# Wider modulation products on VectorE, and a final norm worked by column groups, in a two-layer diffusion trunk

## The chip, the cores and the metric

The kernel runs on one core of one Trainium2 chip. The metric is the device time of one execution in microseconds (us). The time of the kernel before is 1545.48 us, the median of three runs.

## The reference, cut to what matters

Two groups of tokens, 128 context tokens (TP) and 256 latent tokens (TS), 384 columns in all (T), pass through two layers with the same weights. D is 1024, so a token's features lie in KD = 8 blocks of 128 partitions. Each layer is

```
m  = modulation(c, w_ada[l], b_ada[l])                  # 9 vectors of 1024 for each of the two groups
x += 0.5 * m[2] * swiglu(norm(x) * (1 + m[1]) + m[0])   # FFN, d_ff 2816
x += m[5] * (mixers(norm(x) * (1 + m[4]) + m[3]) @ w_out)
x += 0.5 * m[8] * swiglu(norm(x) * (1 + m[7]) + m[6])   # FFN
modulation(c) = silu(c) @ w_ada + b_ada                 # c: (1024,) for each group
y = rms_norm(x, final_norm)                             # once, behind the second layer
```

## The kernel before, in words

Activations are held transposed: features on partitions, the 384 tokens as columns, the two groups as column ranges (`GROUPS`). Every large weight tile is loaded into one of five `raw` buffers by a DMA that SyncE's queue issues, split into a high part by ScalarE (L200) and a low part by VectorE (L201), and multiplied by TensorE in three passes (`mm3`, L210). A `raw` buffer is free again when its low part has been written.

An FFN (`ffn`) runs over 22 blocks of the hidden width in two halves of 11: gate and up products (`g`, `u`), an activation, then for each of the 8 output blocks `j` a down product `dn`, an add into `x` (`add_x`, L290), the scaled input of the next sublayer (`scaled`, L264 and L265) and the square for its norm (`Sumsq.add`, L237). A list `SIDE` says beside which of the 38 steps of an FFN the modulation vectors of later sublayers are worked out. One vector is done by TensorE (`ada_pe`), fifteen by VectorE (`ada_dve`): for each of 8 weight tiles `rawada` [128, 1024], loaded through the same five `raw` buffers, VectorE multiplies the tile by silu(c) of both groups, spread over all partitions, and sums along the columns. The products themselves are thrown away into a PSUM tile `junk`; the sums are kept. L174 does this in pieces of 512 columns, four for each tile. The spread silu(c), `requests`, is loaded anew for each of the four FFNs by `requests_of` (L162, activation at L163), into buffers of the group "S" (8 buffers of 512 columns), which the mixers use too.

The mixers of a layer hold their small weights in a buffer `lw` [128, 2048] of their own (L452), read by several streams of the mixers and, ahead of them, by `narrow` (L466), which makes `wkr`.

The order of the instructions on each engine is set when the program is built, by a scheduler that goes by priority (the order of the program text) and by its own model of when operands are ready. Buffers of one tag are handed out again when their last reader is done. The calls that select a ScalarE table by name (`log_exp`, `act_table`) are pinned in program order; where an activation needs another table than the one loaded, a table load is put ahead of it.

The end: `Sumsq.end` (L243) sums the squares over partitions with a product with ones (L245 for the sum of seven blocks, L247 for the last), `rstd_of` takes Ln and Exp (L221, L222) over all 384 columns, L1099 forms `y` for the 8 blocks, and L1101 stores two blocks at a time from SyncE's queue.

Of the kernel before, what the change touches and what calls it, by code (L numbers as in the profile page):

```python
# [15 lines left out]
P = 128  # L16
D = 1024
# [27 lines left out]
def trunk(ctx, tc, a):  # L45
# [108 lines left out]

    requests = {}

    def requests_of():

        for v in range(2):
            for z in range(2):  # L160
                t = slot("S", "req", (512,))
                nc.sync.dma_start(out=t, in_=a["c"][v:v + 1, z * 512:(z + 1) * 512].to_broadcast([P, 512]))  # L162
                S.activation(t, t, AF.Silu)  # L163
                requests[v, z] = t
        yield

    def ada_dve(l, n):

        sums = sb.tile([P, KD, 2, 2], F32, tag="adasum", name=nm("adasum"), bufs=2)
        for k in range(KD):  # L170
            t = load_w(a["w_adaT"][l, n, k], "ada")
            for v in range(2):
                for z in range(2):
                    V.scalar_tensor_tensor(xbank("junk")[:, 0, :], t[:, z * 512:(z + 1) * 512], 1.0, requests[v, z],  # L174
                                           op0=ALU.mult, op1=ALU.mult, accum_out=sums[:, k, v, z:z + 1])
            if k == KD - 1:
                m = mods[l][:, n * 8:(n + 1) * 8, :]
                V.tensor_tensor(m, sums[:, :, :, 0], sums[:, :, :, 1], op=ALU.add)
                V.tensor_tensor(m, m, bada[:, l, n * 8:(n + 1) * 8].unsqueeze(2).to_broadcast([P, KD, 2]), op=ALU.add)
# [39 lines left out]
    def rstd_of(dst, acc, n):  # L219

        S.activation(dst, acc, AF.Ln, bias=epsb, scale=1.0 / n)  # L221
        S.activation(dst, dst, AF.Exp, scale=-0.5)  # L222
        return dst

    class Sumsq:
# [5 lines left out]
        def add(self, k):  # L231
# [3 lines left out]
            else:  # L235
                sq = one("sq")
                S.activation(sq, x[k], AF.Square)  # L237
# [5 lines left out]
        def end(self):  # L243
            b = bank("ms")
            PE.matmul(b[:, :T], ones, self.acc, start=True, stop=not self.apart)  # L245
            if self.apart:
                PE.matmul(b[:, :T], ones, self.last, start=False, stop=True)  # L247
            return rstd_of(sb.tile([P, T], F32, tag="rstd", name=nm("rstd"), bufs=1), b[:, :T], D)
# [39 lines left out]
    def add_x(k, b, gt):  # L288
        for g, cs in GROUPS:
# [3 lines left out]
    def ffn(l, i, rstd, ab, nxt, side, hook=None, given=(), h=None):  # L293
# [7 lines left out]
        for half in range(2):  # L301
# [41 lines left out]
            for j in range(KD):  # L343
# [8 lines left out]
                add_x(j, b, gt)  # L352
# [76 lines left out]
    def mixers(l, rstd, gt, ab, nxt):  # L429
# [22 lines left out]
        lw = sb.tile([P, 2048], F32, tag="lw", name=nm("lw"), bufs=1)  # L452
# [630 lines left out]
    for l in range(NL):  # L1083
# [10 lines left out]
        ssq = ffn(l, 1, rstd, coefs_of(l, 2), before(l + 1, 0), lambda: side(SIDE[2 * l + 1]))  # L1094
# [156 lines left out]
```

## Time and profile before

| what | value |
|---|---|
| time, median of 3 runs | 1545.48 us (1545.38 to 1546.63) |
| profiled execution, its own time | 1547.53 us |
| its span, first to last instruction | 1545.1 us |
| TensorE busy | 1506.9 us, 98% of the span |
| VectorE busy | 1183.4 us, 77% |
| ScalarE busy | 752.6 us, 49% |
| moved by DMA | 257.33 MB, mean 167 GB/s |

All times are on the profile's clock, which starts at the first instruction. A busy share is that of the whole span; the kernel has an opening (0 to 53 us), four FFNs, two mixers and a tail behind the last down product, and each has limits of its own.

### The profile page before, as it was taken

To read this page: it belongs to the slowest core of one execution; us is meant where nothing else is said; L and a number is where in the kernel's file an instruction comes from. 1 tells how busy PE (TensorE), PEld (TensorE's weight loads), DVE (VectorE), ACT (ScalarE), POOL (GpSimd) and SP (SyncE) were. 2 spreads that over 40 slices of the span, in tenths; PEclk is the share of its full clock that TensorE was granted. 3 is DMA by queue.
4 is the path that set the end of the run, shared out by engine and by line. 5 is a ranking of instruction groups with operands and counts; after the bars stand their busy time and mean duration, and the time that the engine had idled before them with its cause. 6 is when DMAs were issued, how large, how long until landed. Compare 5 with 4: busy or idle time off the path is not lost.

```text
span 1545.1 us, 26749 instructions
## 1 busy us (share of the span) xinstructions
PE 1506.9 (98%) x10120; PEld 1423.9 (92%) x10120; DVE 1183.4 (77%) x2683; ACT 752.6 (49%) x1348; POOL 100.1 (6%) x122
## 2 busy tenths in 40 slices
PE   8999999999999999999999999999999999999997
PEld 5999999997778999999989999999877799999996
DVE  5879998969947988987987799785896599544433
ACT  5732333456788642333454323345677874323331
POOL 1000000100221000000100000001014010000001
PEclk9999999999999999999999999999999999999999
DMA  9877766641134465765645576555221255444331
GB/s 368 270 244 226 245 219 198 209 147 61 49 99 141 151 210 185 245 225 167 195 163 168 173 238 233 181 174 164 72 65 54 65 166 176 150 150 143 112 102 60
DMA packets 83025, 257.33 MB, mean 167 GB/s; under 512 B 9680, under 2 KB 11184, under 8 KB 82512
## 3 DMA queue, kind: packets, MB, share of 16 engines
q1 hardware_dynamic: 81744, 254.14, 50.5%
q8 instruction: 80, 1.31, 0.3%
q0 software_dynamic: 1152, 1.48, 0.3%
q14 instruction: 49, 0.40, 0.1%
HBM read 252.53 MB, written 2.26 MB: 165 GB/s over the span
## 4 chain that ended last, share of the span: by engine, by line
PE 83%; DVE 10%; DMA 3%; ACT 3%; issue 2%; SPq 0%; DVEq 0%; ACTq 0%
PE u L210 22%; PE g L210 22%; PE dn L210 19%; PE in L210 8%; PE out L210 3%; DVE junk L174 2%; PE po L424 1%; DMA rawada<-in_w_adaT 1%; PE sc L391 1%; DVE logu L201 1%; PE first L210 1%; DVE hl L265 1%; DVE loin L201 1%; DMA rawgu<-in_w_gu 1%; DVE x L290 1%
## 5 line engine op out<-in xcount | busy, mean ns | idle before, releaser
L174 DVE SCALAR_TENSOR_TENSOR junk<-rawada,req 128x512 f32<-128x512 f32 x480 | 339.3, 707 | 35.3 <-DMA rawada<-in_w_adaT 25.6
L200 ACT ACTIVATE higu<-rawgu 128x1024 fp32r<-128x1024 f32 (+1 forms) x178 | 186.5, 1050 | 289.9 <-PE u L210 92.8
L210 PE MATMUL g<-h,higu 128*128 128x384 f32 x1136 | 290.6, 335 | 2.0 <-ACT g L329 2.0
L210 PE MATMUL u<-h,higu 128*128 128x384 f32 x1136 | 288.7, 334 | 2.1 <-DVE x L290 1.4
L201 DVE TENSOR_TENSOR logu<-rawgu,higu 128x1024 fp32r<-128x1024 f32 (+1 forms) x178 | 215.2, 1211 | 36.3 <-PE g L210 18.6
L210 PE MATMUL dn<-ah,hidn 128*128 128x384 f32 x704 | 236.1, 335 | 0.2 <-ACT hh L264 0.2
L210 PE MATMUL dn<-al,hidn 128*128 128x384 f32 x704 | 235.9, 335 | 0.0
L210 PE MATMUL dn<-ah,lodn 128*128 128x384 f32 x704 | 235.9, 335 | 0.0
L200 ACT ACTIVATE hidn<-rawdn 128x768 fp32r<-128x768 f32 (+1 forms) x128 | 101.4, 792 | 250.9 <-PE dn L210 68.1
L210 PEld LDWEIGHTS g<-h,higu 128*128 128x128 f32 x1136 | 204.6, 188 | 6.0 <-ACT g L329 2.8
L210 PEld LDWEIGHTS u<-h,higu 128*128 128x128 f32 x1136 | 204.7, 188 | 3.4 <-issue 2.1
L210 PE MATMUL g<-h,logu 128*128 128x384 f32 x568 | 189.8, 334 | 0.0
L210 PE MATMUL u<-h,logu 128*128 128x384 f32 x568 | 189.8, 334 | 0.0
L201 DVE TENSOR_TENSOR lodn<-rawdn,hidn 128x768 fp32r<-128x768 f32 (+1 forms) x128 | 113.4, 886 | 30.5 <-issue 17.0
L210 PEld LDWEIGHTS dn<-ah,hidn 128*128 128x128 f32 x704 | 132.1, 188 | 0.5 <-ACT hh L264 0.5
L210 PEld LDWEIGHTS dn<-ah,lodn 128*128 128x128 f32 x704 | 132.1, 188 | 0.0
L210 PEld LDWEIGHTS dn<-al,hidn 128*128 128x128 f32 x704 | 132.1, 188 | 0.0
L239 POOL TENSOR_TENSOR ssq<-ssq,sq 128x384 f32<-128x384 f32 x42 | 46.5, 1106 | 1152.6 <-DVE hl L265 747.3
L210 PE MATMUL in<-hh,hiin 128*128 128x386 f32 x304 | 107.7, 354 | 0.0
L210 PEld LDWEIGHTS g<-h,logu 128*128 128x128 f32 x568 | 106.6, 188 | 0.0
L210 PEld LDWEIGHTS u<-h,logu 128*128 128x128 f32 x568 | 106.6, 188 | 0.0
L210 PE MATMUL in<-hl,hiin 128*128 128x386 f32 x304 | 106.3, 350 | 0.0
(312 smaller groups left out, 2433.7 us busy)
## 6 DMA issues: line engine op xcount, KB each, us to landing
rawgu<-in_w_gu SPq DMA_DIRECT2D x170, 512.0 KB, 4.3
rawada<-in_w_adaT SPq DMA_DIRECT2D x120, 512.0 KB, 3.8
rawdn<-in_w_dn SPq DMA_DIRECT2D x64, 384.0 KB, 3.6
rawdn<-in_w_dn SPq DMA_DIRECT2D x64, 320.0 KB, 3.0
rawin<-in_w_in SPq DMA_DIRECT2D x38, 512.0 KB, 3.7
rawout<-in_w_out SPq DMA_DIRECT2D x32, 256.0 KB, 2.7
ada<-in_w_ada SPq DMA_DIRECT2D x16, 384.0 KB, 7.3
rawada<-in_w_ada SPq DMA_DIRECT2D x8, 512.0 KB, 4.3
```

Source lines behind the costliest of these rows:

```text
L174: V.scalar_tensor_tensor(xbank("junk")[:, 0, :], t[:, z * 512:(z + 1) * 512], 1.0, requests[v, z], op0=ALU.mult, op1=ALU.mult, accum_out=s ...
L200: S.activation(hi, raw, AF.Copy)
L201: V.tensor_tensor(lo, raw, hi, op=ALU.subtract)
L210: i = PE.matmul(out, wt, xt, start=first and n == 0, stop=last and n == 2)
L239: (V if self.n == KD - 1 else G).tensor_tensor(self.acc, self.acc, sq, op=ALU.add)
L265: V.scalar_tensor_tensor(hl[:, k, cs], x[k][:, cs], at[:, k, g:g + 1], hh[:, k, cs], op0=ALU.mult, op1=ALU.subtract)
L290: V.scalar_tensor_tensor(x[k][:, cs], b[:, cs], gt[:, k, g:g + 1], x[k][:, cs], op0=ALU.mult, op1=ALU.add)
L391: PE.matmul(sc[:, u, :nk], q_of(u, blk), k_of(u, blk), start=True, stop=True)
L424: PE.matmul(bo[64 * u:64 * u + 64, :P], v_of(u, kt), pt[:, u, i * P:(i + 1) * P], start=(i == 0), stop=(i == len(kts) - 1))
```

## The change

`requests_of` loads the spread vectors for both groups into one tile of 2048 columns and applies Silu once. This tile has the tag "wide", with one buffer, and the mixers' `lw` takes its buffer from the same tag. L174 multiplies 1024 columns at once, so there are two products for each weight tile, their thrown-away result covers both banks of `junk`, and the addition of the two halves' sums falls away. In the last FFN, the last `add_x` takes the 256 latent columns first, the last square, the ones-products, Ln and Exp go by column group (latent first, Ln and Exp pinned in this order), the first pair of blocks of `y` goes by column group, `y` lies in buffers of the group "H", and the stores alternate between SyncE's and ScalarE's queue, the last pair as two single blocks.

```
+    def wide(s):
+        return sb.tile([P, 2048], F32, tag="wide", name=nm(s), bufs=1)
...
     def requests_of():
+        t = wide("req")
         for v in range(2):
-            for z in range(2):
-                t = slot("S", "req", (512,))
-                nc.sync.dma_start(out=t, in_=a["c"][v:v + 1, z * 512:(z + 1) * 512].to_broadcast([P, 512]))
-                S.activation(t, t, AF.Silu)
-                requests[v, z] = t
+            requests[v] = t[:, v * D:(v + 1) * D]
+            nc.sync.dma_start(out=requests[v], in_=a["c"][v:v + 1, :].to_broadcast([P, D]))
+        S.activation(t, t, AF.Silu)
...
     def ada_dve(l, n):
-        sums = sb.tile([P, KD, 2, 2], F32, tag="adasum", name=nm("adasum"), bufs=2)
+        sums = sb.tile([P, KD, 2], F32, tag="adasum", name=nm("adasum"), bufs=2)
...
             for v in range(2):
-                for z in range(2):
-                    V.scalar_tensor_tensor(xbank("junk")[:, 0, :], t[:, z * 512:(z + 1) * 512], 1.0, requests[v, z],
-                                           op0=ALU.mult, op1=ALU.mult, accum_out=sums[:, k, v, z:z + 1])
+                V.scalar_tensor_tensor(xbank("junk").rearrange("p a b -> p (a b)"), t, 1.0, requests[v],
+                                       op0=ALU.mult, op1=ALU.mult, accum_out=sums[:, k, v:v + 1])
...
-                V.tensor_tensor(m, sums[:, :, :, 0], sums[:, :, :, 1], op=ALU.add)
-                V.tensor_tensor(m, m, bada[:, l, n * 8:(n + 1) * 8].unsqueeze(2).to_broadcast([P, KD, 2]), op=ALU.add)
+                V.tensor_tensor(m, sums, bada[:, l, n * 8:(n + 1) * 8].unsqueeze(2).to_broadcast([P, KD, 2]), op=ALU.add)
...
-    def rstd_of(dst, acc, n):
-        S.activation(dst, acc, AF.Ln, bias=epsb, scale=1.0 / n)
-        S.activation(dst, dst, AF.Exp, scale=-0.5)
+    def rstd_of(dst, acc, n, pinned=False):
+        keep = tc.keep_in_program_order if pinned else lambda i: i
+        keep(S.activation(dst, acc, AF.Ln, bias=epsb, scale=1.0 / n))
+        keep(S.activation(dst, dst, AF.Exp, scale=-0.5))
...
         def add(self, k):
...
-                S.activation(sq, x[k], AF.Square)
+                for _, cs in reversed(GROUPS) if self.apart and self.n == KD - 1 else ((0, slice(0, T)),):
+                    S.activation(sq[:, cs], x[k][:, cs], AF.Square)
         def end(self):
...
+            groups = GROUPS[::-1] if self.apart else ((0, slice(0, T)),)
+            bs = [bank("ms") for _ in groups]
+            for b, (_, cs) in zip(bs, groups):
+                PE.matmul(b[:, cs], ones, self.acc[:, cs], start=True, stop=not self.apart)
+            for b, (_, cs) in zip(bs, groups):
+                if self.apart:
+                    PE.matmul(b[:, cs], ones, self.last[:, cs], start=False, stop=True)
+                rstd_of(rstd[:, cs], b[:, cs], D, self.apart)
...
     def ffn(l, i, rstd, ab, nxt, side, hook=None, given=(), h=None):
...
-                add_x(j, b, gt)
+                add_x(j, b, gt, GROUPS[::-1] if ssq.apart and half == 1 and j == KD - 1 else GROUPS)
...
     def mixers(l, rstd, gt, ab, nxt):
...
-        lw = sb.tile([P, 2048], F32, tag="lw", name=nm("lw"), bufs=1)
+        lw = wide("lw")
...
     rstd = ssq.end()
-    for k in range(KD):
-        if k % 2 == 0:
-            y = slot("M", "y", (2, T))
-        V.scalar_tensor_tensor(y[:, k % 2, :], x[k], fnorm[:, k:k + 1], rstd, op0=ALU.mult, op1=ALU.mult)
-        if k % 2 == 1:
-            nc.sync.dma_start(out=a["o_y"][:, k - 1:k + 1, :], in_=y)
+    y = [slot("H", "y", (2, T)) for _ in range(KD // 2)]
+    for n, cs in ((0, GROUPS[1][1]), (0, GROUPS[0][1]), *((n, slice(0, T)) for n in range(1, KD // 2))):
+        for k in (2 * n, 2 * n + 1):
+            V.scalar_tensor_tensor(y[n][:, k % 2, cs], x[k][:, cs], fnorm[:, k:k + 1], rstd[:, cs],
+                                   op0=ALU.mult, op1=ALU.mult)
+            if n == KD // 2 - 1:
+                (nc.scalar, nc.sync)[k % 2].dma_start(out=a["o_y"][:, k, :], in_=y[n][:, k % 2, :])
+        if n < KD // 2 - 1:
+            (nc.sync, nc.scalar)[n % 2].dma_start(out=a["o_y"][:, 2 * n:2 * n + 2, cs], in_=y[n][:, :, cs])
```

## Rows read from the trace of the kernel before

**Rows 1.** Windows by stage: stretch, length, each engine's busy time (instructions), clock, DMA share, GB/s.

```profile
53.00:310.83 257.83, 255.84 (x1501) 250.67 (x1501) 232.45 (x529) 99.89 (x147) 6.47 (x6) 1.00 0.72 232
...
503.00:785.40 282.40, 278.63 (x1592) 276.45 (x1592) 252.05 (x564) 116.04 (x177) 8.26 (x7) 1.00 0.61 200
785.40:1063.00 277.60, 275.81 (x1579) 274.43 (x1580) 223.35 (x486) 109.88 (x167) 7.50 (x8) 1.00 0.57 186
...
1254.50:1532.75 278.25, 276.67 (x1586) 275.47 (x1586) 150.22 (x274) 105.87 (x154) 7.24 (x7) 1.00 0.41 128
1532.75:1545.10 12.35, 1.89 (x6) 0.66 (x5) 5.07 (x10) 1.62 (x3) 0.00 (x0) 0.73 0.33 128
...
sum 1545.10, PE 1506.94 PEld 1423.87 DVE 1183.37 ACT 752.55 POOL 100.09; mean PE 188.37 PEld 177.98 DVE 147.92 ACT 94.07 POOL 12.51
```

**Rows 2.** TensorE's timeline, matmuls behind idle time: start, length, what [idle before, releaser].

```profile
176.79 0.59 PE L210 MATMUL u<-h,higu 128*128 128x384 f32 x2 [1.43 <-DVE x L290]
...
315.83 0.91 PE L245 MATMUL ms<-ssq,ones 128*128 128x384 f32 x2 [1.31 <-DVE ssq L239]
...
468.98 0.43 PE L424 MATMUL po<-pt,va 128*64 128x128 f32 x2 [1.15 <-ACT pt L420]
...
785.49 0.41 PE L210 MATMUL u<-hh,higu 128*128 128x386 f32 x1 [2.66 <-ACT hh L264]
...
934.09 0.62 PE L210 MATMUL g<-h,higu 128*128 128x384 f32 x2 [1.42 <-ACT g L329]
...
1316.46 0.62 PE L210 MATMUL g<-h,higu 128*128 128x384 f32 x2 [0.56 <-ACT g L329]
```

**Rows 3.** Instructions grouped by line and shape: count, busy us, mean ns, idle before.

```profile
L174 DVE SCALAR_TENSOR_TENSOR junk<-rawada,req 128x512 f32<-128x512 f32 x480 | 339.3, 707 | 35.3 <-DMA rawada<-in_w_adaT 25.6
...
L201 DVE TENSOR_TENSOR logu<-rawgu,higu 128x1024 fp32r<-128x1024 f32 x170 | 207.6, 1223 | 35.5 <-PE g L210 18.6 <-ACT higu L200 11.3 <-issue 5.3
...
L200 ACT ACTIVATE higu<-rawgu 128x1024 fp32r<-128x1024 f32 x170 | 179.9, 1060 | 289.9 <-PE u L210 92.8 <-DMA rawgu<-in_w_gu 85.9 <-issue 59.4
...
L163 ACT ACT_TABLE_LOAD x8 | 10.3, 1283 | 0.1
L163 ACT ACTIVATE req<-req 128x512 f32<-128x512 f32 x16 | 9.8, 626 | 0.5 <-DMA req<-in_c 0.4
```

**Rows 4.** VectorE's timeline at the end of the second FFN.

```profile
773.52 0.69 DVE L174 SCALAR_TENSOR_TENSOR junk<-rawada,req 128x512 f32<-128x512 f32 x1
...
774.30 0.70 DVE L174 SCALAR_TENSOR_TENSOR junk<-rawada,req 128x512 f32<-128x512 f32 x1
...
784.61 0.73 DVE L290 SCALAR_TENSOR_TENSOR x<-dn,G,x 128x128 f32<-128x128 f32 x2
...
793.32 0.16 DVE L271 COPY sh<-g 128x2 f32<-128x2 f32 x1 [5.71 <-PE g L210]
```

**Rows 5.** ScalarE's timeline: a table load in the mixers, and the norm behind the second FFN.

```profile
466.32 1.28 ACT L222 ACT_TABLE_LOAD   x1
...
788.70 0.58 ACT L221 ACTIVATE rstd<-ms,epsb 128x384 f32<-128x384 f32 x1 [2.40 <-PE ms L245]
```

**Rows 6.** The chain that ended last, over the tail: start, length, what.

```profile
1533.12 0.75 DVE x L290 x2
...
1533.96 0.53 ACT sq L237
...
1534.54 0.93 PE ms L247 x2
...
1535.48 0.59 ACT rstd L221
...
1537.80 3.17 DVE y L1099 x6
```

**Rows 7.** DMA issues: queue, count, KB each, median us from issue to landing.

```profile
lw<-in_lw SPq DMA_DIRECT2D x2, 1024.0 KB, 7.3
...
o_y<-y SPq DMA_DIRECT2D x4, 384.0 KB, 2.8
```

More of the change, by code (lines that the diff above doesn't have):

```diff
@@ L243, in end @@
         def end(self):
[L244 to L248, printed above, removed]
+            rstd = sb.tile([P, T], F32, tag="rstd", name=nm("rstd"), bufs=1)
+            groups = GROUPS[::-1] if self.apart else ((0, slice(0, T)),)
[6 more added lines that the diff above has]
+                rstd_of(rstd[:, cs], b[:, cs], D, self.apart)
+            return rstd
     def log_exp():
@@ L286, in hidden, with add_x @@
         return t[:, 0, :], t[:, 1, :]
-    def add_x(k, b, gt):
-        for g, cs in GROUPS:
+    def add_x(k, b, gt, order=GROUPS):
+        for g, cs in order:
             V.scalar_tensor_tensor(x[k][:, cs], b[:, cs], gt[:, k, g:g + 1], x[k][:, cs], op0=ALU.mult, op1=ALU.add)
```

## The prediction

> **What bounds the kernel now.** I read the windows by stage first [rows 1]. The reader is to see in the sum row that TensorE is busy for 1506.94 of 1545.10 us, so that at most 38.2 us of idle TensorE can be won by anything that gives TensorE no less work, and this change takes no product of weight size away. In the rows above it, the idle time by stage is the length less the first busy number: 2.0 us in the first FFN's stretch, 3.8 in the second, 1.8 in the third, 1.6 in the fourth, 10.5 in the tail. The rest, 18.5 us, is the opening and the two mixers. VectorE, which the change relieves, is busy for 232.45 of 257.83 us in the first FFN (90%), 252.05 of 282.40 in the second (89%), 223.35 of 277.60 in the third (80%) and 150.22 of 278.25 in the fourth (54%). It is not the bound over the span, but it is close to full where the modulation is worked out.
>
> Then TensorE's own timeline, for the places where it stood [rows 2]. Five of them lie in an FFN or at its end and follow a VectorE that is behind: 1.43 us at 176.79, where the bank of `u` waits for the late `add_x`; 1.31 at 315.83, where the sum of squares is late; 2.66 at 785.49, where the scaled input of the next FFN is late; 1.42 at 934.09 and 0.56 at 1316.46, where the activation of `g` is late. Their sum is 7.38 us. VectorE's timeline shows why for the largest [rows 4]: the `add_x` of the last block starts at 784.61, and TensorE had begun to wait at 785.49 - 2.66 = 782.83, so the add came after the wait had begun, not before it. The last chain of waits is the tail, where each step follows the one before it [rows 6].
>
> **The products of 1024 columns.** Two products of 512 columns that follow each other start 774.30 - 773.52 = 0.78 us apart [rows 4], the reading of the sum included, while one lasts 0.707 us in the mean over all 480 [rows 3]. No product of 1024 columns is in this trace. The nearest row is the low part L201, also two SBUF operands, 1024 columns: 1.223 us [rows 3]. The 512 columns more cost 1.223 - 0.707 = 0.516 us, so I take 0.78 + 0.516 = 1.296 us for a wide product. One weight tile then costs 2 x 1.296 = 2.59 us in place of 4 x 0.78 = 3.12: 0.53 us less. With 480 / 4 = 120 tiles that is 63 us of VectorE, 40 tiles (21 us) in each of the first two FFNs. The bounds: nothing less, if a result over two banks cost its 512 columns as a second instruction (2 x 1.56); 3.12 - 2 x 1.223 = 0.67 us for each tile, 81 us, if the reading of the sum hid wholly. The addition of two half sums goes too, once for each of 15 vectors, and is too small to count.
>
> VectorE is off TensorE's path in most of these stretches, so the 63 us buy only the five waits. At the end of the second FFN, 8 tiles are multiplied beside the last seven output blocks, so 8 x 0.53 = 4.2 us of backlog go, more than the wait of 2.66; and the `wkr` of the second mixer no longer stands there, since it needs `lw`, which now comes later. At the others the backlog removed is of the size of one to four tiles, 0.5 to 2.1 us. I take two thirds of 7.38: **4.9 us less**. The bounds are 0 (what is then late is the DMA into the `raw` buffers: VectorE already waited 25.6 us for `rawada` [rows 3]) and 7.4.
>
> **The one request tile.** Four activations of 626 ns become one. By L200 and L163 a column of ScalarE costs (1060 - 626) / 512 = 0.85 ns, so 2048 columns take 0.626 + 1536 x 0.00085 = 1.93 us instead of 2.50 [rows 3]. More counts the table: 8 loads of 1.283 us were put ahead of single Silus, all in the mixers, and each sends a later Exp or Ln back for another one [rows 3, 5]. With one Silu for each FFN, two fall into the mixers at most, so six of these loads go, 7.7 us of ScalarE, and some of those that restore Exp. TensorE waited there for ScalarE once in each mixer, 1.15 us at 468.98 behind such a restoring load at 466.32 and its twin in the second layer [rows 2, 5]. I take half of 2 x 1.15: **1.2 us less**; bounds 0 and 2.3.
>
> The Trainium skill, page "ScalarE: Activation LUTs", section "What ACT_TABLE_LOAD costs", gives a switch 1283 ns for the load, which the row shows, and some 1380 ns more for a drain, of which the row's 0.1 us of idle time ahead of eight loads shows nothing [rows 3]. By it each load that goes is worth twice as much, the term would be the full 2.3 us, and the sum 1538.1 us.
>
> **The one buffer.** `req` and `lw` now wait for each other. The mixers' `lw` (7.3 us from issue to landing [rows 7]) can be issued only behind the last product of the FFN ahead. Its first reader, `wkr`, serves the column block of the mixers that follows nine others of 24 products; at the pace of the third FFN, 277.6 / 1579 = 0.176 us for each [rows 1], that is 38 us later. So the load is hidden, by 30 us. What waits behind it on SyncE's queue are the weight tiles of the mixers, which wait for VectorE's low parts anyway. The request tile of the second FFN comes behind the last reader in the first mixer, before that FFN begins: hidden. That of the third FFN is new at a bad place. In the kernel before there were eight "S" buffers, so it was loaded beside the first mixer; now it waits for the last product of the second FFN, which begins at 774.30 [rows 4]. With 2.8 to 7.3 us to landing [rows 7] it is there between 778 and 782 (an estimate), and its Silu can fall in front of the norm's Ln at 788.70. That costs a load and the Silu, 1.28 + 1.93 us, and loads for Ln and for Exp, 2 x 1.28: 5.8 us of ScalarE. In front of Ln, ScalarE idled 2.40 us [rows 5], and behind rstd, VectorE idled 5.71 us up to 793.32 until the first `g` was there [rows 4], so the 5.8 - 2.4 = 3.4 us that are left are hidden if the delay falls on rstd alone. If the Silu stands ahead of the last scaled input, it delays TensorE by up to 3.2 us. Bounds 0 and 3.2; I take **0.7 us more**, nearer to the covered case.
>
> **The tail** [rows 6]. Before: add 0.75, square 0.53, product 0.93, Ln 0.59, Exp like it, then `y`, the last six of which take 3.17 us and end at 1540.97. By groups the chain for the 256 latent columns runs ahead by the 128 others: a third of the add (0.25) and, by the 0.85 ns of a column, 0.11 us each at square, Ln and Exp, and a third of the product (0.3): 0.9 us earlier. But Ln and Exp of the context columns then follow on ScalarE as two more instructions, and the two `y` products become four: 0.28 us (0.78 - 0.516, a VectorE instruction's fixed part) each for two. So the first `y` starts some 0.8 us earlier and the last ends some 0.4 earlier. The last store is of one block, 192 KB, not of 384 KB, which took 2.8 us [rows 7]; I take 0.5 us for the smaller size, with nothing and 1.35 (7.3 - 2.8 us over 640 KB [rows 7], for 192 KB) as bounds. Together **0.9 us less**; bounds 0.3 more, if four short activations cost a fixed part each on the path, and 1.8 less.
>
> The Trainium skill, page "DMA: Bandwidth & Descriptors", section "Issuing engines are not separate DMA queues", says that transfers issued by several engines run on the same 16 DMA engines and save issue time alone. No run here shows stores on two queues. By it the two last blocks in flight share the engines, the 0.5 falls away, the tail gives 0.4, and the sum would be 1539.7 us.
>
> **The sum**: -4.9 - 1.2 + 0.7 - 0.9 = -6.3 us. Against the profiled execution's span of 1545.1 that is 1538.8; its own time was 1547.5, 2.4 us of it outside the span, and would be 1541.2. The median of the runs, 1545.48, lies 2.0 below that execution; I forecast **1539.2 us** for it, 1536 to 1542 for this case alone.
>
> **The rivals.** *The queue, not VectorE, is late (1543.5 us).* The five waits stay, because with five `raw` buffers the next weights still land late (ScalarE waited 85.9 us for `rawgu` [rows 3]), and only the tail and one mixer wait give: 0.9 + 1.15. For it: the DMA share is 0.57 to 0.72 in the first three FFNs [rows 1]. Against: a buffer's release is VectorE's act too, so a faster VectorE frees it sooner.
>
> *The wide product costs as much as two (1544.5 us)*: the change doesn't do what it says, and the tail alone remains. Against: L201 shows that 1024 columns from SBUF cost no more than 512 twice; for it, no row writes them to PSUM.
>
> *The one buffer stops SyncE's queue (1548.5 us).* The queue stands at `lw` or `req` until the last product is done, and the next stage's weights stand behind it. At three places (near 311, 785 and 1063) that costs the 7.3 us of `lw` less the 4.2 us (24 products) of a tile already split: 3 x 3.1 = 9.3 us, less the 6.3. It decides from a hold of more than about one tile's products at each place; less is hidden.
>
> **How the numbers follow.** The forecast case has 0.72; the late queue 0.16; the wide product without gain 0.05; the stopped queue 0.07. A measurement of this kernel can tell 0.2%, 3.1 us: the border is 1542.4. The forecast's own range lies wholly below it; I put 0.02 of the late queue below it as well. Faster 0.74, same 0.19, slower 0.07. The range: with all bounds at their best, 7.4 + 2.3 + 1.8 is 11.5 us less, 1534.0; at the top it takes in the late queue, 1544.0. The stopped queue is left out.
>
> **What would show it.** Right: L174 120 x 2 = 240 instructions near 1.22 us; VectorE busy some 60 us less; the waits at 785 and 934 under 1 us; two or three table loads at L163; the first `y` near 0.8 us sooner after the last down product. Wrong: L174 at 1.4 us or more; TensorE's idle time in the FFNs unchanged with `DMA rawgu` as releaser; a new wait near 311 or 1063 with `lw` or SyncE's queue before it; or a Silu with three table loads between 775 and 790, and TensorE waiting there for more than 2.7 us.

## The result and the profile after

The changed kernel takes 1586.56 us (median of 6 runs, 1583.46 to 1595.68) against 1546.51 for the kernel before on the same chips: a ratio of 1.0266, interval 1.0249 to 1.0282. I forecast 1539.2 us, faster. By the ratio it is 41 us slower. The profiled execution is the slowest of the six, 1595.68 us, 9 us over the median, so the losses by stage read from it below add up to more than 41 us. A stage of a single profile is itself uncertain: two executions of one and the same program, met below, differ by 3.4 us in the first FFN.

The page of the changed kernel, busy time by engine:

```profile
PE 1527.8 (96%) x10124; PEld 1434.3 (90%) x10124; DVE 1131.6 (71%) x2190; ACT 750.9 (47%) x1338; POOL 102.6 (6%) x122
```

VectorE's busy time fell by 51.8 us, from 1183.4 [rows 1] to 1131.6, as the change promises, and TensorE's rose by 20.9 with only four products more (10124 against 10120, those of the tail's column groups). So the question is where TensorE lost the time. Windows cut at the start of each norm's product show it by stage; first the changed kernel (first FFN, first mixer, second FFN, third FFN, second mixer, fourth FFN, tail), columns as in [rows 1]:

```profile
26.60:321.93 295.33, 286.84 (x1693) 274.65 (x1690) 241.80 (x441) 123.62 (x194) 8.57 (x8) 1.00 0.70 233
321.93:528.17 206.24, 196.28 (x1789) 163.63 (x1790) 145.77 (x364) 140.85 (x309) 31.90 (x42) 0.96 0.26 81
528.17:817.45 289.28, 277.82 (x1581) 273.86 (x1580) 229.78 (x391) 115.06 (x172) 8.11 (x6) 1.00 0.60 198
817.45:1107.09 289.64, 281.62 (x1585) 277.47 (x1586) 210.18 (x358) 113.95 (x172) 9.64 (x8) 0.99 0.56 180
1107.09:1310.26 203.17, 193.26 (x1790) 161.03 (x1790) 145.68 (x364) 140.65 (x309) 31.79 (x42) 0.97 0.26 81
1310.26:1582.81 272.55, 271.53 (x1561) 270.81 (x1560) 141.91 (x232) 101.22 (x147) 6.07 (x6) 1.00 0.40 128
1582.81:1593.80 10.99, 1.73 (x9) 1.24 (x8) 5.32 (x12) 2.07 (x6) 0.00 (x0) 0.71 0.38 143
sum 1567.20, PE 1509.09 PEld 1422.69 DVE 1120.45 ACT 737.43 POOL 96.08; mean PE 215.58 PEld 203.24 DVE 160.06 ACT 105.35 POOL 13.73
```

and the same windows of the kernel before, whose groups above were cut elsewhere:

```profile
27.32:315.83 288.51, 284.42 (x1692) 274.32 (x1689) 261.44 (x606) 124.32 (x197) 7.80 (x8) 1.00 0.72 237
315.83:508.69 192.86, 188.25 (x1790) 158.23 (x1791) 144.19 (x364) 145.07 (x318) 33.30 (x42) 1.00 0.31 98
508.69:787.86 279.17, 275.91 (x1580) 274.03 (x1580) 248.57 (x558) 112.47 (x170) 7.09 (x6) 1.00 0.61 200
787.86:1066.54 278.68, 276.99 (x1587) 275.52 (x1587) 224.15 (x488) 111.15 (x169) 7.50 (x8) 1.00 0.57 186
1066.54:1260.13 193.59, 188.23 (x1790) 158.14 (x1790) 145.04 (x364) 142.99 (x314) 31.77 (x42) 1.00 0.27 85
1260.13:1532.92 272.79, 271.76 (x1560) 270.84 (x1560) 144.59 (x265) 101.45 (x147) 6.07 (x6) 1.00 0.41 128
1532.92:1545.10 12.18, 1.72 (x5) 0.49 (x4) 5.07 (x10) 1.62 (x3) 0.00 (x0) 0.73 0.33 130
sum 1517.78, PE 1487.27 PEld 1411.57 DVE 1173.05 ACT 739.08 POOL 93.54; mean PE 212.47 PEld 201.65 DVE 167.58 ACT 105.58 POOL 13.36
```

The first three FFNs lose 6.8, 10.1 and 11.0 us, the mixers 13.4 and 9.6; the fourth FFN, which has only eight modulation tiles, loses nothing, and the tail gains 1.2. Of the 49.4 us, 21.8 are longer busy time and 27.6 idle time. In the mixers 13.1 of the 23.0 us are longer busy time, and that is the clock: 0.96 and 0.97 in the mean where it was 1.00; 4% of 206.24 us is 8.2 us, against 8.0 us more busy time in the first of them. In windows of 10 us the clock fell in two places of the first mixer, right behind its first norm and at its end, and in the second mixer at its end alone.

**VectorE in the FFNs.** Groups by line and shape, which answer to [rows 3]:

```profile
L176 DVE SCALAR_TENSOR_TENSOR junk<-rawada,req 128x1024 f32<-128x1024 f32 x240 | 297.5, 1240 | 130.7 <-DMA rawada<-in_w_adaT 128.6
L211 PE MATMUL u<-h,higu 128*128 128x384 f32 x1136 | 291.3, 336 | 16.0 <-DVE u L338 11.8 <-DVE x L298 4.1
```

A wide product lasts 1.24 us, as reckoned. But VectorE now stands 128.6 us for modulation tiles (25.6 before), and TensorE stands 11.8 us for VectorE's multiply of `u`. VectorE's timeline in the third FFN shows the link, and under it TensorE's next wait:

```profile
989.27 1.23 DVE L176 SCALAR_TENSOR_TENSOR junk<-rawada,req 128x1024 f32<-128x1024 f32 x1 [3.74 <-DMA rawada<-in_w_adaT]
...
990.43 0.55 DVE L338 TENSOR_TENSOR u<-g,u 128x384 f32<-128x384 f32 x1
990.89 1.22 DVE L202 TENSOR_TENSOR logu<-rawgu,higu 128x1024 fp32r<-128x1024 f32 x1
992.03 0.55 DVE L217 TENSOR_TENSOR al<-u,ah 128x384 fp32r<-128x384 f32 x1
992.50 1.23 DVE L176 SCALAR_TENSOR_TENSOR junk<-rawada,req 128x1024 f32<-128x1024 f32 x1
...
993.64 1.22 DVE L202 TENSOR_TENSOR logu<-rawgu,higu 128x1024 fp32r<-128x1024 f32 x1
998.39 1.23 DVE L176 SCALAR_TENSOR_TENSOR junk<-rawada,req 128x1024 f32<-128x1024 f32 x1 [3.53 <-DMA rawada<-in_w_adaT]
```

```profile
1001.48 0.62 PE L211 MATMUL u<-h,higu 128*128 128x384 f32 x2 [1.83 <-DVE u L338]
```

One tile's first product waits 3.74 us for its transfer, and the multiply that frees `u`'s bank stands behind it. The tile's second product comes at 992.50 without a wait. Then the next tile's first one stands, for 3.53 us, ahead of the next `u`, and TensorE waits 1.83 us for that `u`.

**ScalarE at the third FFN.** Its timeline, and under it TensorE's next product:

```profile
812.42 1.28 ACT L167 ACT_TABLE_LOAD   x1 [6.18 <-DMA req<-in_c]
813.72 1.91 ACT L167 ACTIVATE req<-req 128x2048 f32<-128x2048 f32 x1
815.53 0.78 ACT L272 ACTIVATE hh<-x,A 128x128 fp32r<-128x128 f32 x2
```

```profile
817.45 1.65 PE L251 MATMUL ms<-ssq,ones 128*128 128x384 f32 x2 [5.96 <-DVE ssq L242]
```

ScalarE stood 6.18 us for the broadcast, with the last scaled input behind the Silu. TensorE's wait there was 2.66 us before [rows 2]. The granted clock is 0.63 from 815 to 819 us, the end of the wait included, and 0.51 from 819 to 823, close to the lower of the two levels (1.2 GHz).

**ScalarE in the mixers.** The Silu of the second FFN's request, and the end of the stretch:

```profile
460.49 1.28 ACT L167 ACT_TABLE_LOAD   x1
461.79 1.92 ACT L167 ACTIVATE req<-req 128x2048 f32<-128x2048 f32 x1
...
464.41 1.28 ACT L412 ACT_TABLE_LOAD   x1
...
473.76 1.28 ACT L223 ACT_TABLE_LOAD   x1
...
475.66 1.28 ACT L224 ACT_TABLE_LOAD   x1
...
477.49 1.28 ACT L223 ACT_TABLE_LOAD   x1
...
479.80 1.28 ACT L224 ACT_TABLE_LOAD   x1
```

```profile
466.81 0.44 PE L753 MATMUL bo<-scs,vn 128*64 128x128 f32 x4 [1.87 <-ACT vn L548]
...
479.42 0.55 PE L427 MATMUL tr<-c_first,p 128*128 128x128 f32 x3 [2.34 <-ACT so L223]
482.05 0.69 PE L432 MATMUL po<-pt,va 128*64 128x128 f32 x2 [1.55 <-ACT pt L428]
```

One Silu's load and its 1.9 us come where TensorE needs ScalarE, the Exp at L412 needs a load behind it, and then four loads follow, since the two norms of `so` take Ln and Exp in turn. TensorE stands three times. All loads together number 35, against 36 before: those for Silu fell from eight [rows 3] to three, and those that bring back Ln or Exp (L223, L224, L412) rose from twelve to sixteen.

**VectorE at the mixers' weights.** It stood in order for `lw` at the first reader, `wkr`, twice:

```profile
313.86 0.76 DVE L474 TENSOR_TENSOR wkr<-lw,A 128x256 f32<-128x256 f32 x2 [3.65 <-DMA lw<-in_lw]
...
1085.12 0.43 DVE L474 TENSOR_TENSOR wkr<-lw,A 128x256 f32<-128x256 f32 x1 [5.22 <-DMA lw<-in_lw]
```

After the first of them the norm's product waited 2.92 us, 1.31 before [rows 2]. And the clock fell behind it: 0.66 in the mean from 320 to 330 us, where the kernel before was granted 1.00. The first 40 products from the norm's on took 10.1 us to their last start, against 7.3 before. So this place cost 1.6 us of wait and 2.8 us of clock. In no kernel with `lw` in a buffer of its own did the norm's product wait more than 1.33 us there. After the second wait for `lw` TensorE stood 0.78 us, and not at the norm.

### The profile page after: what moved, and what is told of

It is laid out like the page before. It is cut to its first block, busy times and chain, and to the rows that moved or that the text cites. A ratio compares the mean times of both kernels' runs of the same rounds, so it can differ in the third digit from the quotient of the medians.

```text
span 1593.8 us, 26261 instructions
## 1 busy us (share of the span) xinstructions
PE 1527.8 (96%) x10124; PEld 1434.3 (90%) x10124; DVE 1131.6 (71%) x2190; ACT 750.9 (47%) x1338; POOL 102.6 (6%) x122
## 3 DMA queue, kind: packets, MB, share of 16 engines
q8 instruction: 80, 1.31, 0.3%
## 4 chain that ended last, share of the span: by engine, by line
PE 53%; DMA 18%; DVE 18%; issue 6%; ACT 4%; SPq 0%; DVEq 0%; ACTq 0%
DMA rawada<-in_w_adaT 14%; PE u L211 13%; PE g L211 13%; PE dn L211 9%; PE in L211 8%; DVE junk L176 6%; PE out L211 3%; DVE logu L202 2%; PE po L432 1%; DVE lodn L202 1%; DMA rawgu<-in_w_gu 1%; DMA rawdn<-in_w_dn 1%; PE first L211 1%; PE sc L399 1%; DVE loin L202 1%
## 5 line engine op out<-in xcount | busy, mean ns | idle before, releaser
L176 DVE SCALAR_TENSOR_TENSOR junk<-rawada,req 128x1024 f32<-128x1024 f32 x240 | 297.5, 1240 | 130.7 <-DMA rawada<-in_w_adaT 128.6
L211 PE MATMUL u<-h,higu 128*128 128x384 f32 x1136 | 291.3, 336 | 16.0 <-DVE u L338 11.8
L242 POOL TENSOR_TENSOR ssq<-ssq,sq 128x384 f32<-128x384 f32 x42 | 50.4, 1199 | 1183.2 <-DVE hl L273 778.0
L211 PE MATMUL in<-hh,loin 128*128 128x386 f32 x304 | 107.5, 354 | 0.0
```

The costliest lines, as they stand in the source:

```text
L176: V.scalar_tensor_tensor(xbank("junk").rearrange("p a b -> p (a b)"), t, 1.0, requests[v], op0=ALU.mult, op1=ALU.mult, accum_out=sums[:, k ...
L211: i = PE.matmul(out, wt, xt, start=first and n == 0, stop=last and n == 2)
L242: (V if self.n == KD - 1 else G).tensor_tensor(self.acc, self.acc, sq, op=ALU.add)
```

## The experiments

Ratios are to the kernel before on the same chip, with their intervals. Lines of code are of the kernels named. Stage times come from one profiled execution of each kernel.

### The tail alone

The kernel before with the new `rstd_of`, `Sumsq`, `add_x` order and stores, and nothing of the modulation.

> The kernel before with the tail part alone (column groups, stores on two queues); the modulation stays at 512 columns with four requests in their own slots. The changed kernel's tail was 1.2 us shorter than before (10.99 against 12.18 us from the start of the norm's product). Theory A (the tail is independent of the modulation): 1545.3 us, 1.2 us under the kernel before of the same runs, no new waits before 1530 us. Rival B (the tail's row order and the y buffers in the H slots disturb the planner's order earlier on): slower by 2 us or more, with the loss before 1530 us.

Measured: 1547.06 us against 1547.93, ratio 0.9990 (0.9974 to 1.0005). The tail took 11.0 us (12.18 before), and the other stages lie within 2.1 us of those before. Rival B (2 us or more slower) is excluded by the interval; theory A agrees with the trace, but its 1.2 us are less than the 0.2% that a comparison can tell.

### The width with a request tile of its own

```
-                t = slot("S", "req", (512,))
+        t = sb.tile([P, D], F32, tag="req", name=nm("req"), bufs=1)
-    NSLOT = {"H": 14, "M": 8, "S": 8}
+    NSLOT = {"H": 13, "M": 8, "S": 8}
-        row = sb.tile([P, 256], F32, tag="adarow", name=nm("adarow"), bufs=1)
+        row = one("adarow")[:, :256]
```

These kernels leave out the second condition vector: both column groups use the request of the first, so that it fits in a tile of its own. The first of the three was meant as the control with 512 columns, but it held the 1024-column products by a slip of mine. It is the same program as the second, so the two are a repetition and the first expectation was not tested; the third is the real control.

> Leaves out the second condition vector: both column groups use the first one's request, so that one 1024-column request fits in a tile of its own (nothing is shared with the mixers' weights; one of 14 H slots and the modulation's row buffer are given up for it). The products stay at 512 columns. It is the control for the next kernel. Both theories: as the kernel before within 3 us (1543 to 1550), since VectorE's instructions are the same.

> The same as the control (second condition vector left out, request in a tile of its own), with the products 1024 columns wide. Theory W (the width itself hurts: VectorE, now less loaded, is sent to a modulation tile before it has landed and stands there with the release of u's bank behind it): 15 to 25 us slower than the control, VectorE idle for modulation tiles above 100 us against about 26 us before, the loss in the FFN stages. Rival S (the loss comes from the buffer that is shared with the mixers' weights): 3 to 6 us faster than the control.

> The real control of the two runs before it: second condition vector left out, request in a tile of its own, 13 H slots, products at 512 columns (four per modulation tile). Theory W (width): within 5 us of the kernel before, so 15 to 20 us faster than the same kernel with 1024 columns; its FFN stages as before (288, 279, 279 us). Rival M (the memory that was given up, or one request instead of four, costs the 20 us): 1565 to 1570 us, the FFN stages 5 us longer as with 1024 columns.

Measured with 1024 columns: 1.0137 (1.0112 to 1.0162) and 1.0136 (1.0114 to 1.0157); with 512: 1.0092 (1.0076 to 1.0109). So the width costs some 0.0044 of 1546.5, 7 us, and theory W (15 to 25 us) has the sign and at most half of the size. The repetition's first FFN took 293.8 and 297.2 us, which is how far one stage of one profile can be off. The control itself lies 14 us over the kernel before, against both theories: with 13 H slots each mixer took 197 us (193 before), TensorE waiting 2.5 and 2.2 us for `qk`, and in the first FFN it stood 3.7 us for the modulation's row, which had lost its own buffer. So theory W's 1543 to 1550 for it was wrong, and rival M is right in part. VectorE's wait for modulation tiles was 24.3 us with 512 columns and 125.9 with 1024, the same contrast as between the kernels before and after, without any shared buffer.

### The shared buffer with products of 512

The four slots, each with a Silu of its own, become one tile with one Silu.

```
-                t = slot("S", "req", (512,))
+        t = wide("req")
-        lw = sb.tile([P, 2048], F32, tag="lw", name=nm("lw"), bufs=1)
+        lw = wide("lw")
```

> The kernel before with the requests in one 2048-column tile that shares its buffer with the mixers' weights, as in the changed kernel, but with the products still at 512 columns and the old tail. Theory W (width): at most 20 us slower, and that in the mixers and around the third FFN's request alone, the FFN stages otherwise within 2 us of before. Rival S (shared buffer): 35 to 45 us slower, nearly the whole loss.

Measured: 1573.64 us, ratio 1.0170 (1.0146 to 1.0194), 26 us, between theory W's 20 and rival S's 35. The first FFN took 289.2 us and the fourth 273.5, as before; the mixers 203.6 and 200.9; the second FFN 284.6 with a wait of 4.73 us ahead of the norm's product at its end. In both mixers TensorE stands at the same three places as in the changed kernel, by 1.9, 2.4 and 1.6 us. So the loss has two parts, and each appears alone.

### The Silu and the products kept in place

`keep_in_program_order` holds an instruction, on its own engine, behind those that the program text has ahead of it.

```
-        S.activation(t, t, AF.Silu)
+        tc.keep_in_program_order(S.activation(t, t, AF.Silu))
...
-                V.scalar_tensor_tensor(xbank("junk").rearrange("p a b -> p (a b)"), t, 1.0, requests[v],
-                                       op0=ALU.mult, op1=ALU.mult, accum_out=sums[:, k, v:v + 1])
+                tc.keep_in_program_order(V.scalar_tensor_tensor(
+                    xbank("junk").rearrange("p a b -> p (a b)"), t, 1.0, requests[v],
+                    op0=ALU.mult, op1=ALU.mult, accum_out=sums[:, k, v:v + 1]))
```

The first run has the products' edit alone, on the kernel with its own request tile; the second the Silu's alone, on the changed kernel; the third both.

> The kernel with its own request tile and 1024-column products (second condition vector left out), with each product kept behind what is written before it in VectorE's order, so that the product of one place stands behind that place's multiply of u and split of a. Theory W-order (the width hurts only through VectorE's order: the product is put ahead of work that was ready, and stands there for its transfer): 5 to 15 us faster than without the pins, the idle time of VectorE for modulation tiles under 60 us, the stalls of TensorE for u gone. Rival (the transfers themselves are late because the raw buffers turn over too slowly): within 4 us of the unpinned one.

> The changed kernel with the requests' Silu kept behind what is written before it in ScalarE's order, so that it can run neither in the mixers nor ahead of the last scaled inputs of the second FFN. Theory T (ScalarE's Silu in the wrong place, with its table loads and its wait for the broadcast, is what the shared buffer costs): the stalls of 1.9, 2.3 and 1.6 us in each mixer and the 6.0 us ahead of the third FFN go, and with them the stretches at half clock: 15 to 25 us faster than the changed kernel, about 1563 to 1572 us. Rival L (it is the late load of the mixers' weights, for which VectorE stands 3.7 and 5.2 us, and what follows from it): under 5 us faster.

> The changed kernel with the Silu and the products both kept behind what is written before them. If both causes hold and add up: 25 to 40 us faster than the changed kernel, 1546 to 1562 us, so near the kernel before. If only Silu's place matters: as the kernel with the Silu alone kept, within 4 us.

Silu kept: 1565.76 us, ratio 1.0127 (1.0104 to 1.0150), so 0.0139 of 1546.5, 21.5 us, off the changed kernel's loss. Theory T holds, rival L does not. The table loads fall from 35 to 16. The mixers take 196.1 and 192.5 us, and the three stalls at the end of each are gone; so is the wait ahead of the third FFN's norm. The two windows of the first mixer where the clock had fallen, in this kernel:

```profile
320.00:330.00 10.00, 7.54 (x26) 6.94 (x27) 4.64 (x9) 5.24 (x9) 0.00 (x0) 0.66 0.52 157
480.00:490.00 10.00, 10.00 (x69) 9.03 (x69) 6.23 (x14) 4.56 (x9) 0.54 (x1) 1.00 0.37 118
```

against, in the changed kernel:

```profile
320.00:330.00 10.00, 8.07 (x28) 7.47 (x29) 4.12 (x8) 4.71 (x8) 0.00 (x0) 0.66 0.51 156
480.00:490.00 10.00, 8.45 (x49) 6.33 (x47) 5.29 (x15) 6.08 (x14) 0.59 (x1) 0.66 0.01 2
```

What the Silu cost at the mixer's end is gone. What the wait for `lw` costs at its start stays, and the first mixer stays 3.2 us longer than before.

Products kept everywhere: 1.0190 (1.0169 to 1.0212) with the own tile, 1.0166 (1.0136 to 1.0196) on top of the kept Silu, slower than the same kernels without by 0.0054 and 0.0039, some 8 and 6 us; the intervals of the second pair overlap. My expectation was wrong: VectorE's wait for modulation tiles is gone (2.2 and 2.4 us are left of all its idle time there), but the first FFN takes 307.7 and 306.0 us. TensorE now stands for the down weights' low part instead, 10.0 and 8.7 us in all. I took this to mean that a place that is right in the gate and up half is wrong in the down half; the run with the order by halves, below, doesn't bear that out for the first FFN.

### The width in the changed kernel's own layout, and the order by halves

```
-                V.scalar_tensor_tensor(xbank("junk").rearrange("p a b -> p (a b)"), t, 1.0, requests[v],
-                                       op0=ALU.mult, op1=ALU.mult, accum_out=sums[:, k, v:v + 1])
+                for z in range(2):
+                    V.scalar_tensor_tensor(xbank("junk")[:, 0, :], t[:, z * 512:(z + 1) * 512], 1.0, requests[v][:, z * 512:(z + 1) * 512],
+                                           op0=ALU.mult, op1=ALU.mult, accum_out=sums[:, k, v, z:z + 1])
```

> The changed kernel (shared buffer, new tail) with Silu kept in place and the products at 512 columns again: the width control in the changed kernel's own memory layout. Theory: what is left beside the width is only the late load of the mixers' weights (2 to 5 us): 1546 to 1552 us, 13 to 20 us under the same kernel with 1024 columns (1565.8). Rival (the width costs little, the shared buffer the rest): 1560 us or more.

Measured: 1553.21 us, ratio 1.0036 (1.0024 to 1.0049), against 1.0127 with 1024 columns: 0.0091 of 1546.5, 14 us, is the width's cost, by stages 7.0 us in the first FFN (289.1 against 296.1), 0.8 in the second, 6.1 in the third. Another 2.0 us of the difference lie in the first mixer, where the wait ahead of the norm is 2.42 us and the clock recovers sooner. The total is 1 us above what the theory gave, and the difference, 12.6 us by the medians, at its lower edge; the rival does not hold. Groups of the kernel with 1024 columns and the kept Silu:

```profile
L176 DVE SCALAR_TENSOR_TENSOR junk<-rawada,req 128x1024 f32<-128x1024 f32 x240 | 298.1, 1242 | 122.6 <-DMA rawada<-in_w_adaT 118.5 <-ACT req L167 1.7
L211 PE MATMUL u<-h,higu 128*128 128x384 f32 x1136 | 291.1, 336 | 13.4 <-DVE u L338 10.1 <-DVE x L298 3.2
```

and of the same with 512:

```profile
L177 DVE SCALAR_TENSOR_TENSOR junk<-rawada,req 128x512 f32<-128x512 f32 x480 | 340.6, 710 | 33.1 <-DMA rawada<-in_w_adaT 21.8 <-ACT req L167 1.7
L213 PE MATMUL u<-h,higu 128*128 128x384 f32 x1136 | 290.5, 336 | 4.4 <-DVE x L300 2.5 <-DVE u L340 1.9
```

The second kernel's timeline in the third FFN:

```profile
951.27 0.70 DVE L177 SCALAR_TENSOR_TENSOR junk<-rawada,req 128x512 f32<-128x512 f32 x1
...
952.07 0.70 DVE L177 SCALAR_TENSOR_TENSOR junk<-rawada,req 128x512 f32<-128x512 f32 x1
...
952.86 0.70 DVE L177 SCALAR_TENSOR_TENSOR junk<-rawada,req 128x512 f32<-128x512 f32 x1
...
953.48 1.22 DVE L204 TENSOR_TENSOR logu<-rawgu,higu 128x1024 fp32r<-128x1024 f32 x1
954.61 0.69 DVE L177 SCALAR_TENSOR_TENSOR junk<-rawada,req 128x512 f32<-128x512 f32 x1
...
955.23 0.55 DVE L340 TENSOR_TENSOR u<-g,u 128x384 f32<-128x384 f32 x1
```

Four pieces of one tile fill the time up to `u`'s multiply, and the fourth, just ahead of it, needs a tile that has long landed. With two wide pieces the place ahead of `u` goes to the next tile's first product.

Next, the changed kernel with Silu kept and 1024 columns again, the products kept in order in the gate and up halves alone (`phase[0]` is set at the head of each and cleared at the head of the down products):

```
-                V.scalar_tensor_tensor(
+                (tc.keep_in_program_order if phase[0] else lambda i: i)(V.scalar_tensor_tensor(
```

> The changed kernel with Silu kept in place, and the 1024-column products kept behind what is written before them in the FFNs' gate and up half-stages alone (not in the down products, where the fully pinned kernel stood for lodn). In the changed kernel the first product of the next modulation tile stands right ahead of u's multiply; here both products of a tile follow the split of a. Theory O (that order is the width's whole cost in the FFNs): the first three FFN stages within 2 us of before (288, 279, 279 us), in all 1548 to 1556 us, 10 us or more under the kernel with the Silu alone kept (1565.8). Rival B (the five raw weight buffers turn over too slowly whatever the order, so that a product moved back only makes the next weight tile late): 1563 to 1572 us, with TensorE's waits for logu or lodn in place of those for u.

Measured: 1565.75 us, ratio 1.0115 (1.0097 to 1.0133), not told apart from the kept Silu alone. By stages: the third FFN 279.9 us (283.1 without), the second 282.3 (283.1), but the first 306.1 (296.1), where TensorE stood nine times for `lodn`, 7.1 us. Theory O's total (1548 to 1556 us) failed; its order helps in the third FFN, with 32 modulation tiles, while rival B describes the first, with 40.

And the kept Silus on the kernel before, with the new tail:

> The kernel before with the new tail and the four requests' Silus kept behind what is written before them, so that none runs in the mixers; products at 512 columns, requests in their own slots. Theory T: the table loads in the mixers (a stall of 1.15 us each) and the 2.7 us ahead of the third FFN shrink, and the tail gives its 1.2 us: 2 to 5 us under the kernel before, 1541 to 1545 us. Rival (requests that are ready later make VectorE's products bunch): within 2 us of the kernel before or slower.

Measured: 1551.13 us, ratio 1.0027 (1.0015 to 1.0039): the rival. The mixers' stall of 1.15 us is gone, but the mixers took 193.4 and 193.3 us against 193.7 and 193.6 with the tail alone. The second FFN took 281.7 us and the fourth 274.2, 3.2 and 2.2 longer than there. These are the stages that are longer in the shared kernel with 512 columns too (282.3 and 274.8). Against the tail alone the late Silus cost 0.0037, 5.7 us, and the shared kernel with 512 columns (1.0036) can't be told from this one (1.0027). So most of the 5.6 us that were left there is likely the price of the late Silu, not of `lw`. What makes a late Silu cost that was not traced.

### A sixth weight buffer

```
-        t = sb.tile([P, 1024], F32, tag="raw", name=nm("raw" + s), bufs=5)
+        t = sb.tile([P, 1024], F32, tag="raw", name=nm("raw" + s), bufs=6)
```

> The kernel with Silu and the gate and up products kept in order, with six raw weight buffers in place of five (13 H slots in place of 14, and the modulation's row among the one-row buffers, pay for it). In the first FFN it stood for lodn seven times and that stage took 306.2 us. Theory R (there the raw buffers bind: a product that stands behind the split holds a weight tile's buffer, and the down weights come late): the first FFN falls to 296 us or less and the waits for lodn go. Theory O (order alone): 304 us or more.

> The changed kernel with Silu alone kept in order and six raw weight buffers, paid for in the same way. Theory R (the product waits for a transfer that started late because its buffer came free late): VectorE's idle time for modulation tiles falls from 118 us to under 60 us and the first FFN from 296.1 us to 291 us or less. Theory O (the planner sets the first product of the next tile ahead of u's multiply whenever it takes the tile as landed, so that an earlier start of the load is used up by an earlier place in the order): idle time above 90 us, first FFN within 2 us of 296.1.

> The control of the two: the changed kernel with Silu kept in order, 13 H slots, the modulation's row among the one-row buffers, and still five raw buffers. From the runs with a request tile of its own, which had the same slots: 3 to 4 us longer in the first FFN and in each mixer than with 14 H slots, so 1570 to 1577 us; VectorE's idle time for modulation tiles as with 14 (110 to 125 us).

Measured: with the order kept in the gate and up halves 1557.49 us, ratio 1.0074 (1.0056 to 1.0091), and the first FFN at 289.8 us, the third at 277.7. With the sixth buffer and no order 1.0151 (1.0129 to 1.0172), first FFN 295.6 us, and VectorE's wait unchanged, 122.0 us. The control 1.0168 (1.0153 to 1.0183), first FFN 294.5 us. The control's total is the expected one, but its first FFN is 1.6 us shorter than with 14 H slots, not 3 to 4 longer. So a sixth buffer alone gives nothing in the first FFN, the order alone loses there (with 14 H slots), and both together take back nearly all of the 7 us. Over the whole kernel both together are 0.0094 faster than the control, 14.5 us, about what the width cost; the sixth buffer alone is not told apart from it. The group of the first of the three kernels:

```profile
L177 DVE SCALAR_TENSOR_TENSOR junk<-rawada,req 128x1024 f32<-128x1024 f32 x240 | 296.9, 1237 | 2.2
```

Still it is not faster than the kernel before: with 13 H slots the mixers took 196.5 and 196.9 us (192.9 and 193.6 before), and the second and fourth FFN are 3.1 and 3.8 us longer. The gate and up order with 13 H slots and five buffers was not run. No version beats the kernel before by more than can be measured; the tail alone is the one that does not lose.

## Why the prediction was wrong

**The products' cost: right.** 1.24 us each, 240 of them; two in a row start 999.72 - 998.39 = 1.33 us apart in the trace, where I took 1.296. VectorE's busy time fell by 51.8 us, where I had 63.

**The five waits, 4.9 us less: the step that failed first.** I took them as a backlog of VectorE that shrinks with its work, and put the late transfer at a gain of nothing. But VectorE takes its instructions in order, and the order was made anew with the shorter list. In it the first product of a tile that had not landed came ahead of the multiply that frees `u`. Of the five waits, the 1.43 us became 0.81 and the two for `g` went, but the two ahead of the norms grew from 1.31 and 2.66 to 2.92 and 5.96, and 11.8 us of waits for VectorE's multiply of `u` came. The width's cost is 14 us the other way (1.0127 against 1.0036), 7 us with the request in its own tile; some 2 of the 14 lie in the first mixer, behind the wait for `lw`. The runs show the order and the five buffers as its two conditions: changing either alone won nothing, changing both won 14.5 us. Why the scheduler's model took these tiles as landed is not shown.

**The table loads, 1.2 us less: the wrong sign.** I counted loads and not their place. Five of Silu's eight loads went, near the six that I took, but four more that bring back Ln or Exp came, so 35 are left of 36. The one Silu of the shared tile came behind the last reader of `lw`, at the end of the mixer, where TensorE waits for ScalarE. TensorE's stalls there are 1.87 + 2.34 + 1.55 us against 1.15 [rows 2], and the clock fell behind them. Even with its own 1.15 us gone the kernel before gained only 0.3 us in each mixer, and 5.7 us were lost elsewhere.

By the Trainium skill's page "ScalarE: Activation LUTs", section "What ACT_TABLE_LOAD costs", each switch also pays a drain of some 1380 ns. No run shows it: ScalarE idled 0.1 us in all ahead of the seven loads at L223, and behind the load of 1.28 us at 812.42 the Silu starts at 813.72.

**The third FFN's request, 0.7 us more with a bound of 3.2: mis-sized.** The place was named, and the Silu did stand ahead of the last scaled input. But I charged its load and its 1.9 us alone, and not the 6.18 us for which ScalarE stood for the broadcast, in order. I had the tile there 4 to 8 us behind the start of the last product; that product starts at 798.46, the second of the two broadcasts is issued at 803.70, behind weight tiles on the same queue, and lands at 812.35, 14 us behind. TensorE's wait grew by 5.96 - 2.66 = 3.3 us, and then it ran at half clock.

**"The load is hidden, by 30 us": wrong.** I put the first reader of `lw` where the mixers need its result. VectorE took it as soon as its turn came, and stood 3.65 and 5.22 us. At the first norm that cost 1.6 us of wait and 2.8 us of half clock. No run has the wide products with `lw` in a buffer of its own and the Silu kept, so its share of the whole is not measured.

**The tail, 0.9 us less: right by the trace**, 1.2; the times can't tell it. The first `y` began 1585.75 - 1583.01 = 2.74 us after the last add, where it had been 1536.65 - 1533.12 = 3.53. The Trainium skill's page "DMA: Bandwidth & Descriptors", section "Issuing engines are not separate DMA queues", says that two issuing engines do not double the engines behind them. The trace does not contradict it: the last two stores, of 192 KB on two queues, landed in 2.3 and 2.2 us, where one of 384 KB took 2.8 [rows 7].

**The rivals.** The late queue was the nearest, in that a transfer is what was late, but it was priced at no loss. The wide product without gain is excluded by its 1.24 us. The stopped queue was right that the shared buffer delays the mixers, but SyncE's queue stood only 1.0 us at the first `lw`: it was VectorE that stood. None of the rivals had VectorE's order as a thing that the change itself makes anew. Two of the signs that I had named for being wrong came true: a new wait near the first norm with `lw` before it, and a Silu with three table loads ahead of the third FFN.

Placing the loss by the ratios: 21.5 us by the place of the Silu, 14.1 by the width, 5.6 left. These steps follow one another from the changed kernel down, so they add up to the whole by construction, and that is no check. The other order is one: from the kernel with the shared buffer and 512 columns, with the tail's 0.0010 allowed for, the width costs 0.0106, 16 us, and the Silu's place 0.0124, 19 us, near the same.

## What to carry to other kernels

Where a scheduler orders instructions by its own model of time, a shorter instruction makes a new order. So ask which instruction will now stand ahead of the one that TensorE waits for, and whether its data will have landed by then. When two tiles come to share a buffer, find the first reader and the last by their place in the engine's order, not by where the result is needed, and count the activation tables that the later load drags along. A part that is worth 0.1% is best taken alone, not with a part that moves everything else.

## What the runs showed of the hardware

A VectorE product over two PSUM banks, 1024 columns, costs 1.24 us where 512 cost 0.707: no price for the second bank was seen. The broadcast of one vector to 128 partitions, 512 KB, took 6.2 us from issue to landing in the median and 7.9 beside weight tiles at the third FFN, where modulation tiles of 512 KB took 4.2. And the clock: after a wait of 2.66 us at the end of the second FFN the kernel before kept 1.00, and at the same place the own-tile kernel with 512 columns, after one of 2.63 us (`u` at 795.48), was granted 0.57:

```profile
785.00:789.00 4.00, 3.51 (x18) 3.27 (x19) 2.60 (x5) 1.60 (x4) 0.00 (x0) 1.00 0.65 206
```

```profile
795.00:799.00 4.00, 3.52 (x12) 3.55 (x13) 2.95 (x5) 3.98 (x6) 0.00 (x0) 0.57 0.75 241
```

In the changed kernel it fell behind the waits of 2.92 and 5.96 us. So the cost of a stall is not its own length alone, and from the length alone these rows do not tell whether the clock will fall.
